# Squared-ReLU MLP of a hybrid decoder layer: up-projection by Strassen's scheme, in three passes over the tokens

## The chip, the cores and the metric

The kernel runs on one core of a Trainium2 chip. The metric is the device time of one execution in microseconds, smaller is better. Engines that matter here: PE (TensorE, matmuls; each has its own weight load, PEld), DVE (VectorE), ACT (ScalarE), POOL (GpSimd), and SP, whose queue issues nearly all DMA transfers. Each engine runs its own list of instructions in order, and semaphores tie the lists together.

## The reference, cut to what matters

2048 prompt tokens (with 16 meta tokens in front that are dropped from the output) and 8 sample tokens go through one layer of width D = 1024. The change touches the last two lines of the layer and the final norm:

```python
h = h + jnp.concatenate([y_hg, y_cv], axis=-1) @ w_out
hn2 = _rmsnorm(h, norm2_g)
h = h + jnp.square(jax.nn.relu(hn2 @ w_up)) @ w_down      # w_up 1024x4096, w_down 4096x1024
y = _rmsnorm(h, final_g)
```

All of it is fp32. The kernel keeps to that precision by splitting each operand into a high part that the matmul takes exactly (type fp32r) and the remainder, and by adding three products: high x high, high x low, low x high. So one fp32 block product of 128 x 128 weights costs three matmuls, each with its own weight load.

## The kernel before, in words

**Phase one** (to about 973 us of the span): input projection, gated recurrence, convolution and output projection, for four quarters of the tokens. Its last eight units are the output projection of quarter 3 (`plan_out(3)`, L746). Each unit's epilogue (`out_epilogue`, L1368) adds the residual to the sums in PSUM, and `out_store` (L1322) writes rows of h to DRAM (`hscr`), squares them on ACT and adds the squares on POOL; a few small matmuls then give the mean square of each token.

**Phase two, the MLP** (`plan_mlp`, L705) works on two halves of the tokens: 1032 columns (1024 and the 8 samples) in three blocks of 344, then 1024 in two of 512. Activations lie transposed, features on partitions and tokens along the free dimension. D_FF is cut in eight chunks of 512. A chunk has four up units (8 slices of the inner dimension x 3 products x blocks) and eight down units (4 x 3 x blocks). Where the last chunk of a half is reached, `LASTB` (L703) cuts its blocks anew so that the finish of the first columns starts early.

The norm's token factor is not applied to the operand: since relu squared is homogeneous, the kernel multiplies the residual by the mean square instead (`acc_init`, L1460: `acc` starts as h times `msb`), adds the down products to it, and corrects in the final norm (`finish`, L1472: transposes on PE, squares on ACT, an inverse square root by small one-column DVE operations, two multiplications by gains, a store; `finish_last`, L1501, does the last two tiles). `up_epilogue` (L1586) makes relu and square and both halves of `hid`; `down_epilogue` (L1600) adds a PSUM unit to `acc` on DVE.

`h_prep` (L769) loads a slice of h, multiplies by the gain, and splits it (ACT high, DVE low) into `hT`. For the first half it is added to the background at the start of quarter 2's out units (L1414), for the second half behind the last up unit of the first half (L1660), ahead of that half's last down units.

**Weights** come in pieces of 1 MB (`w_of`, three buffers `wsp0` to `wsp2`). In the first half each piece is loaded raw, split (ACT high, POOL low, `split_to`, L631) and stored to DRAM (`kw`); in the second half it is reloaded split.

**Order.** Units are issued in the order of `plan`. Between the slices of a unit a scheduler (`Background`, `bg.step`) issues background steps: each generator (`h_prep`, `finish`, `acc_init`, ...) yields the engine that it needs next, and the step is taken up when a planner's model of the engines' times says that it is due. The order on each engine is thus fixed when the program is built.

## Time and profile before

| | us |
|---|---|
| median of 3 runs (lowest, highest) | 2449.05 (2447.9, 2450.72) |
| profiled execution | 2447.64 |
| its span | 2445.7 |
| PE busy | 2352.7 (96%) |
| DVE busy | 1171.4 (48%) |
| ACT busy | 683.4 (28%) |
| POOL busy | 520.7 (21%) |

How to read it: every instruction is recorded by one helper (L146), so groups are told apart by tile names (`ps` is PSUM, `act` and later `op0`, `op1`, `extra` hold the operands of the up-projection, `acc` the sums, `wsp` weights, `stat` and `kept` the small columns of an inverse square root). "out<-in" names what is written and read. Matmuls overlap, so a mean of 320 ns is the time from start to end of one, not the distance between two.

### The profile page before, as it was taken

Reading aid. Unit: us, or ns where it says so; the run is one execution under the profiler, and the core shown is the slowest. Engines: PE = TensorE matmul, PEld = TensorE weight load, DVE = VectorE, ACT = ScalarE, POOL = GpSimd, SP = SyncE. Lnnn points to the kernel's source line nnn. Section 1 sums busy time; section 2 is a strip of 40 time slices with the busy share of each in tenths; the row PEclk is TensorE's granted clock in tenths of the full one; section 3 lists DMA queues with packets and bytes.
Section 4 is the critical chain, followed back from the end, with each engine's and each line's share of the span. In section 5 each row is a group of like instructions: output and inputs, shape, how many; then the busy total and the mean of one; then the engine's idle time right before and its main releaser. Section 6 shows DMA issues by size and latency. Waiting matters only on the chain.

```text
span 2445.7 us, 31621 instructions
## 1 busy us (share of the span) xinstructions
PE 2352.7 (96%) x13000; PEld 2100.7 (86%) x13000; DVE 1171.4 (48%) x2003; ACT 683.4 (28%) x1239; POOL 520.7 (21%) x326
## 2 busy tenths in 40 slices
PE   8887898989999999999999999999999999999998
PEld 8887777967887788999999999999888888888887
DVE  6798978587659653523323323326722212222225
ACT  6443644463345333212212211213301100100112
POOL 4562414442237112222212212211000000000000
PEclk9889999999999999999999999999999999999999
DMA  9665454944474468644444444448522222222222
GB/s 300 201 215 175 153 192 139 307 165 167 168 248 159 144 233 294 232 155 141 130 150 135 138 147 140 136 153 304 216 94 95 94 98 92 98 92 98 92 93 97
DMA packets 159221, 396.27 MB, mean 162 GB/s; under 512 B 8772, under 2 KB 107657, under 8 KB 125278
## 3 DMA queue, kind: packets, MB, share of 16 engines
q1 hardware_dynamic: 158934, 394.00, 47.5%
q8 instruction: 102, 1.67, 0.3%
q14 instruction: 41, 0.34, 0.0%
q10 hardware_dynamic: 144, 0.26, 0.0%
HBM read 265.91 MB, written 128.79 MB: 161 GB/s over the span
## 4 chain that ended last, share of the span: by engine, by line
PE 73%; DVE 6%; ACT 1%; DMA 1%; issue 0%; POOL 0%; SPq 0%; ACTq 0%; POOLq 0%; DVEq 0%
PE ps L146 73%; DVE ps L146 3%; DVE stat L146 1%; ACT scr L146 0%; DVE kept L146 0%; DMA scr<-xscr 0%; DVE I L146 0%; DMA wsp<-kw 0%; POOL scr L146 0%; DVE act L146 0%; DVE scr L146 0%; DVE glu L146 0%; DVE B L146 0%; DVE xn L146 0%; ACT act L146 0%
## 5 line engine op out<-in xcount | busy, mean ns | idle before, releaser
L146 PE MATMUL ps<-act,wsp 128*128 128x512 f32 (+5 forms) x7704 | 1504.6, 354 | 8.8 <-POOL wsp L146 4.3
L146 PEld LDWEIGHTS ps<-act,wsp 128*128 128x128 f32 x7704 | 1284.4, 191 | 171.2 <-POOL wsp L146 4.9
L146 PE MATMUL ps<-hid,wsp 128*128 128x344 f32 (+4 forms) x3864 | 713.0, 345 | 1.6 <-DMA wsp<-kw 1.6
L146 PEld LDWEIGHTS ps<-hid,wsp 128*128 128x128 f32 x3864 | 646.4, 188 | 64.0 <-issue 1.8
L146 DVE TENSOR_TENSOR acc<-ps,acc 128x1032 f32<-128x1032 f32 (+5 forms) x160 | 162.0, 1013 | 467.4 <-PE ps L146 467.3
L146 POOL TENSOR_TENSOR wsp<-raw,wsp 128x1024 fp32r<-128x1024 f32 (+1 forms) x98 | 235.6, 2404 | 611.4 <-ACT wsp L146 575.8
L146 DVE TENSOR_TENSOR xn<-xn 128x1032 f32<-128x1032 f32 (+3 forms) x68 | 80.3, 1180 | 509.3 <-ACT hid L146 509.3
L146 ACT ACTIVATE xn<-ps 128x1032 f32<-128x1032 f32 (+5 forms) x74 | 69.2, 935 | 835.1 <-PE ps L146 832.3
L146 POOL TENSOR_TENSOR scr<-scr 128x512 f32<-128x512 f32 x172 | 227.8, 1325 | 266.8 <-ACT scr L146 241.8
L146 DVE SCALAR_TENSOR_TENSOR ps<-glu,cw,ps 128x512 f32<-128x512 f32 x292 | 219.5, 752 | 5.8
L146 ACT ACTIVATE wsp<-raw 128x1024 fp32r<-128x1024 f32 (+1 forms) x98 | 101.6, 1037 | 299.8 <-PE ps L146 216.0
L146 DVE TENSOR_TENSOR hid<-xn,hid 128x1032 fp32r<-128x1032 f32 (+3 forms) x68 | 133.5, 1963 | 2.3
L146 ACT ACTIVATE scr<-glu,cw 128x512 f32<-128x512 f32 x188 | 125.7, 715 | 2.0 <-DVE glu L146 2.0
L146 DVE TENSOR_TENSOR scr<-ps,scr 128x512 f32<-128x512 f32 x48 | 32.8, 684 | 81.1 <-DMA scr<-xscr 55.8
L146 ACT ACTIVATE hid<-xn 128x1032 fp32r<-128x1032 f32 (+3 forms) x68 | 69.0, 1015 | 2.2
L146 ACT ACTIVATE junk<-ps 128x128 bf16<-128x128 f32 (+3 forms) x100 | 38.3, 383 | 108.4 <-PE ps L146 95.2
L146 POOL TENSOR_TENSOR fg<-fg 128x512 f32<-128x512 f32 x28 | 36.6, 1307 | 97.7 <-ACT fg L146 97.7
L146 DVE RECIPROCAL I<-B 128x512 f32<-128x512 f32 (+1 forms) x16 | 54.0, 3378 | 0.5
L146 DVE SCALAR_TENSOR_TENSOR stat<-stat,kept 128x4 f32<-128x4 f32 (+4 forms) x144 | 41.8, 291 | 3.3
L146 DVE TENSOR_TENSOR act<-scr,act 128x512 fp32r<-128x512 f32 (+1 forms) x30 | 23.7, 791 | 37.7 <-ACT act L146 37.6
L146 PE MATMUL ps<-ident,scr 128*128 128x128 f32 (+1 forms) x148 | 22.1, 282 | 17.8 <-ACT scr L146 17.8
L146 DVE TENSOR_TENSOR stat<-stat,kept 128x4 f32<-128x4 f32 (+4 forms) x144 | 37.6, 261 | 3.4
(189 smaller groups left out, 1192.1 us busy)
## 6 DMA issues: line engine op xcount, KB each, us to landing
wsp<-kw SPq DMA_DIRECT2D x167, 1024.0 KB, 4.8
kw<-wsp SPq DMA_DIRECT2D x96, 1024.0 KB, 5.6
raw<-in_w_up_dram SPq DMA_DIRECT2D x32, 512.0 KB, 6.5
raw<-in_w_down_dram SPq DMA_DIRECT2D x32, 512.0 KB, 6.0
raw<-in_w_in_dram SPq DMA_DIRECT2D x24, 512.0 KB, 7.9
out_dram<-xn SPq DMA_DIRECT2D x18, 512.0 KB, 4.4
scr<-xscr SPq DMA_DIRECT2D x32, 256.0 KB, 7.2
hscr<-scr SPq DMA_DIRECT2D x32, 256.0 KB, 7.1
```

The costliest lines, as they stand in the source:

```text
L146: return fn(*args, **kw)
```

## The change

**Three passes.** Tokens go in three passes of 688, 688 and 680 columns (`T0`, `PN`), each split in two halves of 344 or 340 columns. D_FF goes in 16 groups of 256.

**Seven products.** In a group, w_up is a 2 x 2 matrix of blocks (two halves of D, two halves of the group's 256 columns) and the tokens' operand another (two halves of D, two halves of the pass). Strassen's scheme (Winograd's form) replaces eight block products by seven, P1 to P7, each 4 slices x 3 matmuls. S1 to S4 are sums of blocks of w_up, T1 to T4 sums of blocks of h. `up_epilogue` puts the four output blocks together in `cst` by DVE additions (P5 is held in PSUM bank 1 until P7), then makes relu and square and `hid`.

**Weight sums every pass.** Per group `up_prep` loads four raw blocks, makes four sums, and splits seven blocks: seven high parts on ACT, five low parts on DVE, two on POOL, into a ring of nine slots. `up_first` does this for the first group during the out units of quarter 3; six of its steps come after the out-projection. Down weights are split in pass 0 (ACT, POOL), stored, and reloaded in passes 1 and 2.

**Token sums.** `h_prep(p, i)` (i = 0 to 3) loads slices i and i + 4 of the pass, makes the four sums and splits seven blocks into single buffers (`op0`, `op1`, `extra`), through two stages (`bst0`, `bst1`) that it shares with `up_prep`. For pass 0 it is added at the start of quarter 3's out units, i = 2 and 3 go through `acc`, and need the memory of phase one; for passes 1 and 2 it waits for the last product of the pass before.

**Order.** Middle groups alternate products and down units (U0 D0 U1 D1 ... U6 D6 D7, the D's of the group before). The first group of a pass has seven products in a row; the last one ends with 13 down units in a row.

**Residual and norm.** The first group's down units are copied to `acc` by ACT. The residual h times mean square is added in the background during the pass (`residual`: a load, a POOL multiplication, a DVE addition for each of eight slices). Mean squares go through DRAM (`mscr`), and the column for the final norm is gathered by 20 small transfers (`eps_cols`). All six finish tiles of a pass wait for the last down unit of the pass; in the last pass the last down units run in two sweeps of 424 and 256 columns, and `finish_last` does the last two tiles.

```diff
+    NPASS, NG = 3, DFF // 256
+    T0 = [0, 680, 1368]
+    PROMPT = [680, 688, 680]
+    PN = [688, 688, 680]
...
+    PRODUCTS = [("P1", "A11", 0, B11), ("P5", "S1", 1, T1), ("P6", "S2", 2, T2), ("P3", "S4", 0, B22),
+                ("P7", "S3", 2, T3), ("P2", "A12", 0, B21), ("P4", "A22", 2, T4)]
...
+                (4, 0, "dve", total("S3", "A11", "S1", ALU.subtract)), (4, 0, "dve", total("S1", "S1", "A22", ALU.add)),
+                (4, 0, "act", hi("A11")), (5, 0, "dve", total("S2", "S1", "A11", ALU.subtract)),
+                (5, 0, "dve", total("S4", "A12", "S2", ALU.subtract)), (5, 0, "act", hi("A22")),
+                (6, 0, "dve", lo("A11", V)), (6, 0, "act", hi("A12")), (7, 0, "pool", lo("A22", G)),
+                (7, 1, "act", hi("S4")), (8, 1, "dve", lo("S4", V)), (9, 2, "act", hi("S3")),
+                (9, 0, "pool", lo("A12", G)), (10, 2, "dve", lo("S3", V)), (11, 5, "act", hi("S1")),
+                (12, 5, "dve", lo("S1", V)), (13, 6, "act", hi("S2")), (13, 6, "dve", lo("S2", V))]
...
+    def up_first():
+        steps = up_prep(0)
+        late = (20, 21, 13, 14, 15, 17)
+        got = yield from take(bstage, 2)
+        for n_ in [n_ for n_ in range(len(steps)) if n_ not in late] + list(late):
+            if n_ == late[0]:
...
+                bstage.give(*got)
+                yield from until(("mix",))
...
+    def h_prep(p, i):
+
+        n = PN[p] // 2
+        yield from until(*[("h", q, d) for q in quarters(p) for d in (i, i + 4)])
+        if p == 0:
+            yield from region(i // 2, 4)
+        else:
+            yield from until(("up", p - 1))
+        if p == 0 and i < 2:
+            raws = yield from take(xns, 2)
...
+        st_ = yield from take1(bstage)
...
+        lo_scaled(B11, r[B11], g)
+        lo_(T1, s1)
+        lo_(T2, s2)
+        done.add(("bop", p, i, 0))
...
+                G.tensor_tensor(t[:, 0:n], t[:, 0:n], msb[:, 0:n], ALU.mult)
...
+                V.tensor_tensor(acc[:, k, 0:n], acc[:, k, 0:n], t[:, 0:n], ALU.add)
...
+            yield from until(("emm",), *[("res", p, k) for k in range(K8)])
...
+            r_ = yield from rsqrt(ss, 1, 1.0 / D, parts=n, eps=emm[:n, p, i:i + 1])
...
+            if name == "P1":
+                S.activation(c11, src, AF.Copy)
+            elif name == "P6":
+                V.tensor_tensor(c21, src, c11, ALU.add)
+                V.tensor_tensor(c12, held, c21, ALU.add)
+            elif name == "P3":
+                V.tensor_tensor(c12, src, c12, ALU.add)
+                ready(c12, a, 1)
+            elif name == "P7":
+                V.tensor_tensor(c21, src, c21, ALU.add)
+                V.tensor_tensor(c22, held, c21, ALU.add)
+                ready(c22, b, 1)
...
+                if g == 0:
+                    bg.wait(done, ("bop", p, i, idx // 3))
+                for wl, xl in ((0, 0), (0, 1), (1, 0)):
+                    mctx.t = 0.0
+                    T.matmul(ps[:, bank_, 0:n], lhsT=w[:, wl, i * P:(i + 1) * P], rhs=bop(i, xl, idx)[:, 0, 0:n],
+                             start=(i == 0 and wl == 0 and xl == 0), stop=(i == 3 and wl == 1))
...
+        def down(p, g, d, bl, outs, w):
+            m = len(outs)
+            n = (bl[1] - bl[0]) // m
+            mctx.e = "pe"
+            for k in range(2):
+                for wl, xl in ((0, 0), (0, 1), (1, 0)):
+                    lhs = w[:, wl, k * P:(k + 1) * P]
+                    for h in range(m):
+                        mctx.t = 0.0
+                        c0_ = bl[0] + h * n
+                        T.matmul(outs[h], lhsT=lhs, rhs=hid[g % 2][k][:, xl, c0_:c0_ + n],
+                                 start=(k == 0 and wl == 0 and xl == 0), stop=(k == 1 and wl == 1))
...
+                    bg.until(lambda: all(("fin", p - 1, i) in done for i in range(6)))
+                S.activation(a, view_, AF.Copy)
+                done.add(("acc", p, d))
+            else:
+                V.tensor_tensor(a, view_, a, ALU.add)
...
+            seq += U_(0, range(7))
+            for g in range(1, NG):
+                ds = [D_(g - 1, d) for d in range(K8)]
+                us = U_(g, range(7))
+                if g == 1:
+                    seq += us[0:3] + [x for i in range(4) for x in (ds[i], us[3 + i])] + ds[4:]
+                elif g == NG - 1:
+                    seq += [us[0], ds[0], us[1], us[2], ds[1], us[3], us[4], ds[2], us[5], us[6]] + ds[3:]
+                else:
+                    seq += [x for i in range(7) for x in (us[i], ds[i])] + ds[7:]
+            bls = [whole] if p < NPASS - 1 else [(0, 424), (424, 680)]
+            seq += [D_(NG - 1, d, bl) for bl in bls for d in range(K8)]
```

What the change does to the order, at three places. First DVE where the out-projection ends. `scr<-ps` is the eviction of an out unit; `act<-xn` before, and `op0<-xn` after, are low parts of the up operand; `bst` are stages, `ups` and `wsp` weights of the first group, `fg<-ps` the mean square of quarter 3. Before:

```order
L146 TENSOR_TENSOR scr_111<-ps_96,scr_111 128x512 [waits DMAHW0_49,PE_49]
L146 TENSOR_TENSOR scr_111<-ps_96,scr_111 128x512 [waits DMAHW3_49,PE_49]
L146 TENSOR_TENSOR scr_111<-ps_96,scr_111 128x512 [waits DMAHW6_49,PE_49]
L146 TENSOR_TENSOR scr_111<-ps_96,scr_111 128x512 [waits DMAHW1_49,PE_49,Pool_49]
L146 SCALAR_TENSOR_TENSOR act_83<-xn2_91,vec_70,act_83 128x1032 [waits Activation_49]
L146 SCALAR_TENSOR_TENSOR act_83<-xn0_89,vec_70,act_83 128x1032 [waits Activation_49]
L146 SCALAR_TENSOR_TENSOR act_83<-xn1_90,vec_70,act_83 128x1032 [waits DMAHW4_49,Activation_49]
L146 SCALAR_TENSOR_TENSOR act_83<-xn3_92,vec_70,act_83 128x1032 [waits DMAHW7_49,Activation_49]
```

After:

```order
L146 TENSOR_TENSOR scr_115<-ps_93,scr_115 128x512 [waits DMAHW3_49,PE_49]
L146 TENSOR_TENSOR ups3_7385<-raw0_84,ups3_7385 128x512 [waits Activation_49]
L146 TENSOR_TENSOR wsp1_87<-raw0_84,wsp1_87 128x512 [waits DMAHW5_49,Activation_49]
L146 SCALAR_TENSOR_TENSOR bst0_7386<-xn3_114,ng2_78,bst0_7386 128x344 [waits DVE_49,Activation_49,Pool_49]
L146 SCALAR_TENSOR_TENSOR bst0_7386<-xn1_90,vec_70,bst0_7386 128x336 [waits DMAHW2_49,DVE_49]
L146 TENSOR_TENSOR bst0_7386<-kept_76,bst0_7386 128x8 [waits Activation_49]
L146 TENSOR_SCALAR fg_91<-ps_93 1x512 [waits PE_49]
L146 TENSOR_TENSOR wsp1_87<-raw1_85,wsp1_87 128x512 [waits Activation_49]
L146 SCALAR_TENSOR_TENSOR bst1_7387<-xn0_89,ng2_78,bst1_7387 128x344 [waits Activation_49]
L146 SCALAR_TENSOR_TENSOR bst1_7387<-xn2_113,vec_70,bst1_7387 128x336 [waits DMAHW4_49,DVE_49]
L146 TENSOR_TENSOR bst1_7387<-kept_76,bst1_7387 128x8 [waits Activation_49]
L146 SCALAR_TENSOR_TENSOR op0_82<-xn3_114,vec_70,op0_82 128x344
```

The four preparations that stood in one piece behind the last eviction are replaced by a chain of sums and splits, of which the first low part of the first slice is the last row shown, and weight remainders stand among them.

Second, DVE at the end of the first half (before) and of pass 0 (after). `stat` and `kept` are the inverse square root of a finish tile, `xn<-ps` its multiplication by gains. Before:

```order
L146 SCALAR_TENSOR_TENSOR kept_76<-stat_75,kept_76 128x1 [waits DVE_49]
L146 SCALAR_TENSOR_TENSOR stat_75<-stat_75,kept_76 128x1 [waits DVE_49]
L146 TENSOR_TENSOR stat_75<-stat_75,kept_76 128x1 [waits DVE_49]
L146 SCALAR_TENSOR_TENSOR kept_76<-stat_75,kept_76 128x1 [waits DVE_49]
L146 SCALAR_TENSOR_TENSOR stat_75<-stat_75,kept_76 128x1 [waits DVE_49]
L146 TENSOR_TENSOR stat_75<-stat_75,kept_76 128x1 [waits DVE_49]
L146 TENSOR_TENSOR acc_7675<-ps_96,acc_7675 128x384 [waits PE_49]
L146 SCALAR_TENSOR_TENSOR kept_76<-stat_75,kept_76 128x1 [waits DVE_49]
L146 TENSOR_TENSOR kept_76<-kept_76,rs2_78 128x1 [waits DVE_49]
L146 SCALAR_TENSOR_TENSOR xn1_90<-ps_96,kept_76,fg_93 128x512 [waits DMAHW6_49,DVE_49,Pool_49]
L146 SCALAR_TENSOR_TENSOR xn1_90<-ps_96,kept_76,fg_93 128x512
```

After:

```order
L146 SCALAR_TENSOR_TENSOR kept_76<-stat_75,kept_76 128x1 [waits DVE_49]
L146 TENSOR_TENSOR stat_75<-stat_75,kept_76 128x1
L146 SCALAR_TENSOR_TENSOR bst1_7387<-raw0_84,ng2_78,bst1_7387 128x344 [waits DMAHW4_49,Activation_49]
L146 SCALAR_TENSOR_TENSOR bst1_7387<-raw1_85,vec_70,bst1_7387 128x344 [waits DMAHW5_49,DVE_49]
L146 SCALAR_TENSOR_TENSOR stat_75<-stat_75,kept_76 128x1
L146 SCALAR_TENSOR_TENSOR kept_76<-stat_75,kept_76 128x1
L146 TENSOR_TENSOR stat_75<-stat_75,kept_76 128x1 [waits DVE_49]
L146 SCALAR_TENSOR_TENSOR stat_75<-stat_75,kept_76 128x1 [waits DVE_49]
L146 SCALAR_TENSOR_TENSOR kept_76<-stat_75,kept_76 128x1 [waits DVE_49]
L146 SCALAR_TENSOR_TENSOR xn1_90<-ps_93,kept_76,fg_91 128x512 [waits DVE_49,PE_49]
L146 SCALAR_TENSOR_TENSOR xn1_90<-ps_93,kept_76,fg_91 128x512 [waits PE_49]
L146 SCALAR_TENSOR_TENSOR op1_83<-raw0_84,vec_70,op1_83 128x344 [waits Activation_49]
```

Before, adds of the last down units (`acc<-ps`) stand among the small operations; after, sums for the next pass's operand (`bst1<-raw`, `op1<-raw`) stand there, and all adds of the pass are ahead of them.

Third, PE at the end of the program. `ident,acc` are the transposes of finish tiles. Before:

```order
L146 MATMUL ps_96<-hid0_7669,act_83 128x256 [waits DVE_49]
L146 MATMUL ps_96<-hid0_7669,act_83 128x256 x2
L146 MATMUL ps_96<-hid1_7670,act_83 128x256 x3
L146 MATMUL ps_96<-hid2_7671,act_83 128x256 x3
L146 MATMUL ps_96<-hid3_7672,act_83 128x256 x3
L146 MATMUL ps_96<-ident_66,acc_7675 128x128
L146 MATMUL ps_96<-ident_66,acc_7675 128x128 [waits DVE_49]
L146 MATMUL ps_96<-ident_66,acc_7675 128x128 x7
L146 MATMUL ps_96<-ident_66,acc_7675 128x128 [waits DVE_49]
L146 MATMUL ps_96<-ident_66,acc_7675 128x128 x2
L146 MATMUL ps_96<-ident_66,acc_7675 128x128 [waits DVE_49]
L146 MATMUL ps_96<-ident_66,acc_7675 128x128
L146 MATMUL ps_96<-ident_66,acc_7675 128x128 [waits DVE_49] x2
```

After:

```order
L146 MATMUL ps_93<-ident_66,acc_7718 128x128 [waits DVE_49]
L146 MATMUL ps_93<-ident_66,acc_7718 128x128 x3
L146 MATMUL ps_93<-ident_66,acc_7718 128x128 [waits DVE_49]
L146 MATMUL ps_93<-ident_66,acc_7718 128x128 x3
L146 MATMUL ps_93<-ident_66,acc_7718 128x128 [waits DVE_49]
L146 MATMUL ps_93<-ident_66,acc_7718 128x128 x3
L146 MATMUL ps_93<-ident_66,acc_7718 40x128 [waits DVE_49]
L146 MATMUL ps_93<-ident_66,acc_7718 40x128 x3
L146 MATMUL ps_93<-ident_66,acc_7718 40x128 [waits DVE_49]
L146 MATMUL ps_93<-ident_66,acc_7718 40x128 x3
L1991 UNCONDITIONAL_BRANCH
```

Before, the last matmuls with `hid` are followed by 16 transposes, the rest of the last two tiles. After, no matmul with `hid` is near the end: the rows shown end with the eight transposes of a tile of 128 tokens and the eight of the tile of 40 tokens, half a tile at a time behind a wait for DVE.

## Rows read from the trace of the kernel before

**Rows 1.** The page: busy share of each engine; chain that ended last, by engine.
```profile
PE 2352.7 (96%) x13000; PEld 2100.7 (86%) x13000; DVE 1171.4 (48%) x2003; ACT 683.4 (28%) x1239; POOL 520.7 (21%) x326
...
PE 73%; DVE 6%; ACT 1%; DMA 1%; issue 0%; POOL 0%; SPq 0%; ACTq 0%; POOLq 0%; DVEq 0%
```

**Rows 2.** Windows: stretch, length, busy us (x instructions) of PE, PEld, DVE, ACT, POOL, granted clock, DMA.
```profile
970.00:2430.00 1460.00, 1457.94 (x7961) 1326.70 (x7960) 462.98 (x587) 236.94 (x290) 159.15 (x67) 1.00 0.40 135
1100.00:1300.00 200.00, 200.00 (x1269) 200.00 (x1268) 61.90 (x36) 39.00 (x38) 42.14 (x18) 1.00 0.45 139
1800.00:2000.00 200.00, 200.00 (x866) 162.13 (x865) 42.86 (x35) 16.69 (x16) 0.00 (x0) 1.00 0.27 95
```

**Rows 3.** Groups of PE by form: operands, shape xcount, busy us, mean ns, idle before.
```profile
L146 PE MATMUL ps<-act,wsp 128*128 128x344 f32 x2232 | 355.0, 320 | 0.0
L146 PE MATMUL ps<-hid,wsp 128*128 128x512 f32 x1416 | 329.4, 394 | 0.0
```

**Rows 4.** Timeline of ACT, first half: start us, length us; two up units in a row.
```profile
1205.48 1.03 ACT L146 ACTIVATE xn<-ps 128x1032 f32<-128x1032 f32 x1 [8.28 <-PE ps L146]
...
1216.84 1.03 ACT L146 ACTIVATE xn<-ps 128x1032 f32<-128x1032 f32 x1 [8.28 <-PE ps L146]
```

**Rows 5.** Timeline of ACT, second half: two up units in a row.
```profile
1925.77 1.02 ACT L146 ACTIVATE xn<-ps 128x1024 f32<-128x1024 f32 x1 [8.98 <-PE ps L146]
...
1936.86 1.02 ACT L146 ACTIVATE xn<-ps 128x1024 f32<-128x1024 f32 x1 [8.98 <-PE ps L146]
```

**Rows 6.** Groups of DVE by form, 970 us to the end.
```profile
L146 DVE TENSOR_TENSOR hid<-xn,hid 128x1032 fp32r<-128x1032 f32 x31 | 90.2, 2908 | 1.1
L146 DVE TENSOR_TENSOR acc<-ps,acc 128x1032 f32<-128x1032 f32 x56 | 68.9, 1231 | 213.1 <-PE ps L146 213.1
...
L146 DVE TENSOR_TENSOR hid<-xn,hid 128x1024 fp32r<-128x1024 f32 x31 | 38.0, 1225 | 1.1
...
L146 DVE SCALAR_TENSOR_TENSOR xn<-ps,kept,fg 128x512 f32<-128x512 f32 x28 | 19.7, 746 | 1.3 <-DVE kept L146 0.5
...
L146 DVE TENSOR_TENSOR acc<-ps,acc 128x384 f32<-128x384 f32 x16 | 8.8, 553 | 11.5 <-PE ps L146 11.5
...
L146 DVE SCALAR_TENSOR_TENSOR stat<-stat,kept 128x1 f32<-128x1 f32 x42 | 6.6, 157 | 1.0
```

**Rows 7.** Groups of POOL by form, whole span: weight splits of 512 columns.
```profile
L146 POOL TENSOR_TENSOR wsp<-raw,wsp 128x512 fp32r<-128x512 f32 x4 | 5.1, 1283 | 8.3 <-ACT wsp L146 8.2
```

**Rows 8.** DMA issues: count, KB each, us from issue to landing.
```profile
out_dram<-xn SPq DMA_DIRECT2D x18, 512.0 KB, 4.4
...
xn<-hscr SPq DMA_DIRECT2D x16, 512.0 KB, 8.1
```

**Rows 9.** Timeline of DVE where phase one ends and the MLP begins.
```profile
973.39 0.69 DVE L146 TENSOR_TENSOR scr<-ps,scr 128x512 f32<-128x512 f32 x1 [4.92 <-PE ps L146]
974.00 5.94 DVE L146 SCALAR_TENSOR_TENSOR act<-xn,vec,act 128x1032 fp32r<-128x1032 f32 x4
```

**Rows 10.** Timeline of PE where the first half of the tokens ends.
```profile
1705.93 0.85 PE L146 MATMUL ps<-hid,wsp 128*128 128x264 f32 x5 [1.59 <-DMA wsp<-kw]
```

**Rows 11.** Timeline of DVE there: two finish tiles in a row.
```profile
1715.23 0.15 DVE L146 TENSOR_TENSOR stat<-stat 128x1 f32<-128x1 f32 x1
...
1719.53 0.15 DVE L146 TENSOR_TENSOR stat<-stat 128x1 f32<-128x1 f32 x1
```

**Rows 12.** Timeline of PE around a gap in phase one.
```profile
805.55 0.66 PE L146 MATMUL ps<-ident,I 128*128 128x128 f32 x4 [4.50 <-DVE I L146]
```

**Rows 13.** Windows of that gap and of the 4 us behind it.
```profile
800.00:806.00 6.00, 1.50 (x10) 0.98 (x8) 5.82 (x12) 0.20 (x1) 2.63 (x3) 1.00 0.44 172
806.00:810.00 4.00, 4.00 (x17) 3.44 (x16) 3.78 (x7) 0.80 (x2) 0.00 (x0) 0.57 0.00 0
```

**Rows 14.** Timeline of PE at the end.
```profile
2429.17 2.98 PE L146 MATMUL ps<-hid,act 128*128 128x256 f32 x24
2431.99 1.69 PE L146 MATMUL ps<-ident,acc 128*128 128x128 f32 x14
```

More of the change, by code (lines that the diff above doesn't have):

```diff
@@ L1337, in out_store @@
                 if d == K8 - 1:
-                    half, i0 = q // 2, 4 * (q % 2)
                     if q == 0:
@@ new lines, in eps_cols @@
+        def eps_cols():
+            yield "pool"
+            G.memset(emm, 1.0)
+            yield from until(*[("st", q) for q in range(NQ)])
+            yield "sp"
+            for p in range(NPASS):
+                for i, c0_, n in tiles_of(p):
+                    m = min(n, PROMPT[p] - c0_)
+                    a = T0[p] + c0_
+                    SP.dma_start(emm[0:m, p, i:i + 1], mscr[:, a:a + m].rearrange("o p -> p o"))
+                    if m < n:
+                        SP.dma_start(emm[m:n, p, i:i + 1], mscr[:, SEQ:SEQ + NS].rearrange("o p -> p o"))
+            yield "dve"
+            V.scalar_tensor_tensor(out=emm, in0=emm, scalar=EPS, in1=emm, op0=ALU.mult, op1=ALU.mult)
+            done.add(("emm",))
```

639 lines of the change are left out of this document (396 added, 243 removed).

## The prediction

> **What bounds the kernel now.** The page comes first [rows 1]: PE is busy 96% of the span, DVE 48%, and the chain that ended last is 73% PE. Then the windows [rows 2]: from 970 to 2430 us PE is busy 1457.9 of 1460 us at granted clock 1.00 (2.4 GHz), while DVE has 463 us. The MLP is one unbroken stream of matmuls, and only its length counts; DVE and ACT have slack on average. The groups by form [rows 3] show no idle time before these matmuls, so I read their price from the cadence, not from their 320 ns of latency. An up unit of 72 matmuls of 344 columns comes every 1216.84 − 1205.48 = 11.36 us, which is 157.8 ns each [rows 4]; one of 48 of 512 columns every 11.09 us, 231.0 ns each [rows 5]. Both are 0.45 to 0.46 ns per column: columns are paid, not instructions.
>
> The stream runs from the eviction of the last out-projection unit at 973.4 [rows 9] to 2429.17 + 2.98 = 2432.15 [rows 14]: 1458.8 us. The profiled execution took 2447.64 us, 1.4 below the median; its span is 2445.7, so 1.9 lie around it.
>
> **Part by part: the stream.** Before: 4248 matmuls of 344 (670.3 us), 2952 of 512 (681.9), and 600 narrower ones of the last units, 185,280 columns at 0.459 ns (85.0): 1437.2. The other 21.6 of the 1458.8 are 1.6 of waiting for a weight piece [rows 10] and mostly transposes, some 0.12 each [rows 14]. After: 3 passes x 16 groups x (7 products x 12 + 8 down units x 12) = 8640 matmuls: 5760 of 344 (908.9), 2784 of 340 at 156.0 (434.2), and 48 each of 424 and 256 (15.0): 1358.1. **−79.1 us**, an eighth of the up columns.
>
> A rule speaks against this. The Trainium skill, "TensorE: Matmul & The Clock Gate", section "Back-to-back issue gap", gives about 81 ns for sustained 128-column pairs of weight load and matmul, and 131 ns for 512. By it (109 ns at 344, an estimate on a straight line between these) the stream would go from about 910 to 942 us, +32 for −79. The trace disagrees with 157.8 and 231.0.
>
> **The start of the MLP.** Before, the operands of the first up unit are ready when the out-projection ends: DVE's last four preparations take 5.94 us in one piece at 974.0 [rows 9], and PE goes on. After, h_prep cannot take its stages until up_first gives them back, and DVE comes to it only behind the last evictions. From there to the operand that the last quarter of P1 needs, DVE has 24 scalar_tensor_tensors of 336 or 344 columns, 11 tensor_tensors of 344, 5 operations of 512 columns and 10 of 8 columns. By [rows 6] 344 columns cost about 0.515 (384 cost 0.553, 1032 cost 1.231), a scalar_tensor_tensor of 344 about 0.57 (0.746 at 512), 512 columns 0.69, a small one 0.16: 13.7 + 5.7 + 3.5 + 1.6 = 24.5 us against 1.9 us of PE for P1. Moreover the four loads for i = 2, 3 stand on SP behind two stores of down weights, and these wait for POOL's split behind ACT's first preparations, at about 18; a load lands some 8 us later [rows 8] and leaves about 8 us of DVE. That makes some 33, less 1.9, and a little for the second group's sums, which wait for a stage: **+32** (24 by DVE alone, 40 if a second load queues).
>
> **The two pass boundaries.** Before, the second half's operands lie ready and finish tiles spread among adds; the whole boundary cost 1.6 us [rows 10]. After, the next pass may overwrite its operands only once U6 of group 15 is done, and D0 needs a bank pair that the last finish tile gives back. Between the last add of a pass and that tile's gains DVE has, in its order, 16 scalar_tensor_tensors and 21 tensor_tensors of 344, 9 of 512, 12 gains and 78 one-column operations: 9.1 + 10.8 + 6.2 + 9.0 + 12.2 = 47.3 us [rows 6]. These are dependent chains: a tile alone took 4.3 us before [rows 11], so some 3 more. PE has 10 products (18.9) and 48 transposes (5.8) to run meanwhile: 24.7. The first pass also splits down weights on POOL, where a 1032-column subtraction on DVE took 2.91 for 1.23 [rows 6]; that puts DVE late before it begins. **+28** (20 to 36) and **+26** (18 to 34), each with 5.8 of transposes besides.
>
> **Inside the groups.** A group is 7 x 1.89 + 8 x 1.89 = 28.4 us of PE. DVE has 9 sums and remainders of 512 (6.2), 7 adds of products (3.6), 4 remainders of hid (2.1) and 8 adds of 688 columns at 0.875 (7.0): 18.9. POOL's splits in the first pass are at most 7.8, half of 1.28 for 256 columns [rows 7]; even if DVE stood still for all of them, 26.7 fits in 28.4. The residual adds 8 POOL products (1.7 each, by the same row) and 8 DVE adds per pass; they are hidden unless DVE is already late. **+3** (0 to 12) for products that come out of step.
>
> **Clock.** In phase one a gap of 4.5 us [rows 12] was followed by a stretch at granted clock 0.57 [rows 13], mostly at the 1.2 GHz level: 0.43 of 4 us, 1.7 us, are lost. From 970 to 2430 there is none [rows 2]. The new stalls hold gaps of that size at three places, more than one at each: **+6** (0 to 12).
>
> **Tail.** From the last hid matmul to the end of the span it is now 13.5 us. After, the last sweep has 48 matmuls of 256 columns (5.6 us), and DVE four finish tiles (15), eight adds (3.4) and the last two tiles (6.5): 25 us. The last store lands 4.4 later [rows 8]: 25 − 5.6 + 4.4 = **24** (18.5 to 26.5).
>
> **Sum.** 973.4 + 1358.1 + 32 + (28 + 5.8) + (26 + 5.8) + 2.9 (transposes in the last sweep) + 3 + 6 = 2441.0 for the last matmul; + 24 + 1.9 = **2467**, +19 on 2447.6. The saving is real and is more than spent where DVE prepares operands that PE needs at once.
>
> **Rivals.**
> *The boundaries hide more.* If every low end holds (24, 20, 18, no low clock, no wait in groups, tail 18.5), the time is 2467 − 38 = 2429, faster. For it: DVE is only 48% busy, independent operations overlap a little, and before, finish tiles cost PE nothing. Against it: the order on DVE is fixed and its 47 us are counted. It decides for faster once the three stalls together are below some 62 us instead of 86.
> *Waits in the steady state.* If each group's adds come 1 us late, 48 groups give +48 less the 3 counted: 2512. For it: held bank 1 ties two products to one add, and POOL beside DVE is dear [rows 6]. Against it: 18.9 of 28.4. It decides if DVE with POOL's share passes 28.4.
> *Price by instruction.* If a matmul's price were one of instructions, 840 more at 157.8 would be +133 instead of −79: 2679. The 512-column cadence [rows 5] excludes nearly all of it: the slope between [rows 4] and [rows 5] leaves 8 ns per instruction. The rule of the Trainium skill above points this way.
> *The stream alone.* If preparation is covered entirely, 2447.6 − 79 = 2369: the change would do all that its count promises. Against it: h_prep cannot begin before the last product by its own condition.
>
> **How the numbers follow.** Forecast case (2443 to 2500) 0.66, hidden boundaries 0.17, waits 0.13, the stream alone 0.03, price by instruction 0.01. The range leaves out the two last, half of the waits and some of the hidden case: 2430 to 2505. About 0.2% (5 us) is what a measurement can tell: faster 0.18 (below 2442.7), same 0.12, slower 0.70.
>
> **What would show it.** In the changed profile: 157 to 158 ns per matmul in mid-pass; PE idle of some 30 us behind the out-projection with DVE as releaser; two stretches of some 25 us at pass starts where DVE is full and PE is not; low clock there; mid-pass PE at 100%. I am wrong if those stretches are short, if mid-pass PE is below 97%, or if the last matmul ends far from 2441.

## The result, and the profile after

The changed kernel takes 2520.27 us (median of 4 runs, 2515.5 to 2524.6) against 2449.89: a ratio of 1.029 [1.026, 1.031], slower by 70 us. The forecast was slower by 19, with 2505 as its upper end; the direction was right and the size was not. The profiled execution took 2517.8 us, its span is 2516.1.

The page after, against [rows 1]: busy share of each engine, PE and its granted clock in 40 slices, the chain that ended last.

```profile
PE 2317.9 (92%) x13790; PEld 2166.6 (86%) x13790; DVE 1704.1 (68%) x3129; ACT 1056.1 (42%) x2230; POOL 655.1 (26%) x511
...
PE   9887889989999996899999977999999889999996
...
PEclk9898999999999998899999997999999989999998
...
PE 52%; DVE 12%; issue 6%; DMA 4%; ACT 3%; POOL 3%; SPq 1%; DVEq 0%; POOLq 0%; ACTq 0%
```

PE's share of the chain falls from 73% to 52%. Each slice is 63 us long. Behind the first 15, PE's slices dip at three places, the starts of the three passes, and at the end. Windows after, against [rows 2]: group 0 of pass one (passes count from one here, groups from 0 to 15); its groups 5 to 8; start of pass two; its groups 5 to 14; start of pass three.

```profile
985.00:1035.00 50.00, 22.43 (x85) 18.95 (x84) 34.53 (x74) 22.62 (x56) 5.09 (x5) 0.61 0.31 88
1155.00:1270.00 115.00, 112.18 (x706) 111.17 (x707) 77.95 (x114) 50.58 (x112) 40.91 (x40) 1.00 0.49 152
1494.00:1579.00 85.00, 56.78 (x312) 52.89 (x311) 57.91 (x161) 41.50 (x90) 8.11 (x5) 0.80 0.34 113
...
1670.00:1950.00 280.00, 280.00 (x1781) 280.00 (x1780) 175.32 (x278) 100.31 (x196) 25.45 (x20) 1.00 0.38 113
1998.00:2075.00 77.00, 55.59 (x314) 52.64 (x313) 55.12 (x158) 39.05 (x86) 8.13 (x5) 0.80 0.36 109
```

In the middle of pass two PE is as full as before. Its timeline there, units of 12 matmuls (start, length), as [rows 4] was read:

```profile
1755.20 2.06 PE L146 MATMUL ps<-op,wsp 128*128 128x344 f32 x12
...
1770.31 1.89 PE L146 MATMUL ps<-op,ups 128*128 128x344 f32 x11
```

Eight units, 96 matmuls, start in 15.11 us: 157.4 ns per matmul of 344 columns, against 157.8 in [rows 4]. A group of the third pass repeats every 28.0 us, 155.6 ns per matmul of 340. The stream is 5760 x 157.4 + 2784 x 155.6 ns and 15 us for the wide and narrow ones of the last group: 1354.8 us. **The saving on PE is there in full.** What is left of a stretch when its matmuls are taken off at this cadence I call lost; transposes, and the useless matmuls of e11 and e12, count as lost too. A stretch runs from the first matmul of an up unit to that of another; the starts of passes two and three are their first two groups, with 48 transposes (e1 and e3 have none there). "First group" is group 0 of pass one. All in us, each from one profiled execution:

| kernel | first matmul | lost: first group | rest of pass 1 | start of pass 2 | rest of 2 | start of pass 3 | rest of 3 | last group | last matmul |
|---|---|---|---|---|---|---|---|---|---|
| after | 985.5 | 36.4 | 18.8 | 43.8 | 6.7 | 36.0 | 6.2 | 2.7 | 2490.9 |
| e1 no finish | 986.1 | 35.8 | 19.0 | 18.8 | 6.2 | 17.2 | 3.8 | 2.7 | 2444.5 |
| e2 no preparation | 985.0 | 35.5 | 15.9 | 31.7 | 7.2 | 27.6 | 6.1 | 2.6 | 2466.3 |
| e3 neither | 987.6 | 36.4 | 18.2 | 13.2 | 4.4 | 8.1 | 6.0 | 2.7 | 2431.4 |
| e4 eight products | 983.9 | 18.8 | 4.1 | 20.3 | 1.2 | 15.5 | −0.5 | 2.7 | 2491.2 |
| e5 ng2 moved | 982.0 | 37.1 | 18.3 | 42.5 | 8.4 | 36.4 | 6.2 | 2.6 | 2488.4 |
| e6 low part on ACT | 983.3 | 37.5 | 34.6 | 41.8 | 6.6 | 37.4 | 6.1 | 2.6 | 2504.7 |
| e7 loads at the start | 985.4 | 26.0 | 28.9 | 43.5 | 7.6 | 37.2 | 6.0 | 2.6 | 2492.0 |
| e8 sums later | 987.8 | 35.5 | 18.5 | 40.7 | 6.4 | 37.8 | 5.8 | 2.6 | 2489.9 |
| e9 rounding on POOL | 988.0 | 35.0 | 15.5 | 43.5 | 6.6 | 35.8 | 5.8 | 2.7 | 2487.6 |
| e10 no residual | 989.5 | 34.9 | 15.7 | 40.1 | 0.9 | 37.0 | 0.0 | 2.6 | 2475.5 |
| e11 filled gaps | 986.6 | 35.4 | 18.9 | 38.3 | 4.9 | 34.6 | 3.4 | 2.6 | 2479.4 |
| e12 all moves | 982.0 | 24.9 | 20.0 | 35.9 | 5.9 | 35.6 | 2.5 | 2.6 | 2464.2 |
| e13 down weights ready | 987.6 | 30.4 | 2.1 | 37.3 | 8.8 | 36.7 | 4.7 | 2.6 | 2464.8 |

The first column scatters: in the kernels that keep phase one as the change has it, the first matmul comes between 983.3 and 989.5 us.

Rows that show the waits. DVE at the end of phase one, against 973.39 in [rows 9]:

```profile
980.90 0.69 DVE L146 TENSOR_TENSOR scr<-ps,scr 128x512 f32<-128x512 f32 x1 [1.89 <-PE ps L146]
```

PE at the start of the MLP (idle before and who ended it), then at the start of pass two:

```profile
1004.01 0.65 PE L146 MATMUL ps<-op,ups 128*128 128x344 f32 x1 [11.49 <-ACT op L146]
...
1026.44 3.81 PE L146 MATMUL ps<-op,wsp 128*128 128x344 f32 x12 [6.52 <-DVE cst L146]
...
1527.73 3.81 PE L146 MATMUL ps<-op,ups 128*128 128x344 f32 x12 [6.36 <-DVE cst L146]
...
1554.04 3.81 PE L146 MATMUL ps<-hid,wsp 128*128 128x344 f32 x12 [6.79 <-DVE xn L146]
```

The last line is D0 of pass two; its releaser, on DVE, is the gain of the last finish tile:

```profile
1552.59 1.40 DVE L146 SCALAR_TENSOR_TENSOR xn<-ps,kept,fg 48x512 f32<-48x512 f32 x2
```

### The profile page after: what moved, and what is told of

Same layout as the page of the kernel before. It is cut to its first block, busy times and chain, and to the rows that moved or that the text cites. A ratio compares the mean times of both kernels' runs of the same rounds, so it can differ in the third digit from the quotient of the medians.

```text
span 2516.1 us, 37234 instructions
## 1 busy us (share of the span) xinstructions
PE 2317.9 (92%) x13790; PEld 2166.6 (86%) x13790; DVE 1704.1 (68%) x3129; ACT 1056.1 (42%) x2230; POOL 655.1 (26%) x511
## 4 chain that ended last, share of the span: by engine, by line
PE 52%; DVE 12%; issue 6%; DMA 4%; ACT 3%; POOL 3%; SPq 1%; DVEq 0%; POOLq 0%; ACTq 0%
PE ps L146 52%; DVE ps L146 2%; DMA junk<-in_w_down_dram 2%; DVE stat L146 2%; POOL wsp L146 1%; ACT cst L146 1%; SPq L146 1%; DVE op L146 1%; DMA bst<-in_w_up_dram 1%; DVE raw L146 1%; DVE acc L146 1%; DVE xn L146 1%; DVE cst L146 1%; POOL ups L146 1%; ACT wsp L146 1%
## 5 line engine op out<-in xcount | busy, mean ns | idle before, releaser
L146 PE MATMUL ps<-op,wsp 128*128 128x512 f32 (+6 forms) x5427 | 1068.9, 352 | 33.9 <-DVE cst L146 11.4
L146 PEld LDWEIGHTS ps<-op,wsp 128*128 128x128 f32 x5427 | 897.4, 195 | 137.7 <-DVE cst L146 11.1
L146 PE MATMUL ps<-hid,wsp 128*128 128x344 f32 (+1 forms) x4536 | 769.5, 321 | 34.1 <-DVE xn L146 13.8
L146 DVE TENSOR_TENSOR acc<-ps,acc 128x688 f32<-128x688 f32 (+3 forms) x368 | 313.2, 851 | 278.1 <-PE ps L146 277.5
L146 ACT ACTIVATE cst<-cst 128x344 f32<-128x344 f32 (+1 forms) x384 | 188.3, 490 | 507.3 <-DVE cst L146 501.2
L146 PE MATMUL ps<-op,ups 128*128 128x344 f32 (+1 forms) x2013 | 358.3, 326 | 34.0 <-ACT op L146 15.2
L146 PEld LDWEIGHTS ps<-op,ups 128*128 128x128 f32 x2013 | 330.9, 193 | 39.5 <-ACT op L146 16.4
L146 DVE TENSOR_TENSOR cst<-ps,cst 128x344 f32<-128x344 f32 (+1 forms) x336 | 171.1, 509 | 30.6 <-PE ps L146 27.1
L146 DVE TENSOR_TENSOR hid<-cst,hid 128x344 fp32r<-128x344 f32 (+1 forms) x192 | 104.6, 545 | 52.6 <-ACT hid L146 51.6
L146 POOL TENSOR_TENSOR wsp<-raw,wsp 128x1024 fp32r<-128x1024 f32 (+1 forms) x34 | 78.7, 2314 | 79.6 <-ACT wsp L146 68.1
```

The lines of the kernel that those rows point to most:

```text
L146: return fn(*args, **kw)
```

## The experiments

The kernel before was run on the same chip each time: 2451 to 2453 us, 1 to 3 above the 2449.89 of the result. The changed kernel was not run again beside the experiments, so a difference of 3 us or less from its 2520.27 says little.

**e1, e2, e3: what the pass starts are made of.** e1 leaves out the finish tiles of passes one and two:

```diff
-                    bg.until(lambda: all(("fin", p - 1, i) in done for i in range(6)))
...
-            elif g == NG - 1 and d == K8 - 1:
+            elif p == NPASS - 1 and g == NG - 1 and d == K8 - 1:
```

e2 leaves out the operands of passes two and three (those of pass one are used again); e3 does both:

```diff
-                if p < NPASS - 1:
-                    for i in range(4):
-                        bg.add(h_prep(p + 1, i), 1)
+                for i in range(4):
+                    for a_ in range(3):
+                        done.add(("bop", p + 1, i, a_))
```

> The changed kernel without the finish tiles of passes 0 and 1 (their rows of y are not written; the wait of the next pass's first down unit on them goes with them). Theory (DVE's list of operations between the passes sets the boundaries, which cost 49.6 and 42.3 us): 21 to 24 us of DVE and 5.3 of transposes leave each boundary, so each falls by 15 to 22 and the time by 30 to 44, to 2476-2490. Rival (only the preparation of operands counts, finish tiles lie beside it): under 10 us less in all, 2508 or more.

> The changed kernel with the operands of pass 0 used in passes 1 and 2 too (no preparation for these passes; their products are of the wrong tokens). Theory (DVE's list): 24 us of DVE leave each boundary and its first product waits for nothing; what is left is the finish tiles' chain against 10 products, some 8 to 15 us a boundary: 65 to 80 less, 2438-2455. Rival (the wait of the first down unit on the last finish tile decides alone): the boundaries fall by 10 each, about 2500.

> Both left out: no finish tiles in passes 0 and 1 and no operands for passes 1 and 2. Theory: only the wait behind the second group's weight sums is left, some 6 us a boundary: 80 less, about 2440. If the two parts add up, e3's gain is the sum of e1's and e2's; if they stand in one queue where either fills it, e3's gain is less than the sum. Rival (boundaries cost by the low clock or by transfers): over 2470.

Measured: 2473.1, 2495.6 and 2455.1 us. By the table the finish tiles are worth 25.0 and 18.8 us at the two starts, the operands 12.1 and 8.4, both together 30.6 and 27.9. So the work of DVE there is the cause of most of it. Of what the tiles are worth, 5.8 us are their 48 transposes on PE, by the prediction's price; the rest, 19.2 and 13.0, is about one and a half times the operands' share, as the work is: between the last add and the last gain, the tiles take 21.2 us of DVE by the prediction's terms (9.0 + 12.2), and the operands 16 scalar_tensor_tensors and 10 tensor_tensors, 14.3 us. (The prediction has 21 tensor_tensors there; of the 22 in the trace, 12 are adds of products and remainders of `hid`. Its 9 operations of 512 columns are weight sums and low parts of the second group.) e2 was a miss: 25 us less where 65 to 80 were expected, near its rival, since D0 waits for the last tile with or without the operands before it. PE in e2:

```profile
1537.65 3.81 PE L146 MATMUL ps<-hid,wsp 128*128 128x344 f32 x12 [6.86 <-DVE xn L146]
```

e3 came 15 us above its forecast. One long wait stays at each of its starts, 9.33 us in pass two and 4.1 in pass three. PE, then DVE, in pass two:

```profile
1512.64 3.81 PE L146 MATMUL ps<-op,ups 128*128 128x344 f32 x12 [9.33 <-DVE cst L146]
```

```profile
1504.78 0.69 DVE L146 TENSOR_TENSOR raw<-bst,raw 128x512 f32<-128x512 f32 x1 [8.13 <-DMA bst<-in_w_up_dram]
```

DVE is free, but its weight sums for the second group stand in its order ahead of the add that PE waits for, and they wait for loads. Behind the first limit lay a second.

**e4: eight products in the new frame.** The three passes, their operands, finish tiles and residual stay; C11 = A11 B11 + A12 B21 and so on takes the place of Strassen's sums and adds.

```diff
-    UP = ["A11", "A12", "A22", "S1", "S2", "S4", "S3"]
-    PRODUCTS = [("P1", "A11", 0, B11), ("P5", "S1", 1, T1), ("P6", "S2", 2, T2), ("P3", "S4", 0, B22),
-                ("P7", "S3", 2, T3), ("P2", "A12", 0, B21), ("P4", "A22", 2, T4)]
+    UP = ["A11", "A12", "A22", "S1"]
+    PRODUCTS = [("c11a", "A11", 0, B11), ("c11b", "A12", 0, B21), ("c12a", "A11", 1, B12), ("c12b", "A12", 1, B22),
+                ("c21a", "S1", 2, B11), ("c21b", "A22", 2, B21), ("c22a", "S1", 0, B12), ("c22b", "A22", 0, B22)]
```

(S1 holds A21 there.)

> Three passes, 16 groups and the background residual kept, but eight block products a group instead of seven: no sums of weights or tokens, four blocks split instead of seven on either side, products accumulated in PSUM, no additions of products on DVE. PE gets 48 more products (+90.6 us by the measured 157.4 ns). Theory (Strassen's extra work on DVE and ACT is what the boundaries, the start and pass 0 cost): the start falls from 41 to about 18, the boundaries from 50 and 42 to about 25 each, pass 0's waits from 18 to 5: 75 less, so 2510-2550 in all. Rival (three passes cost it, whatever the products): the losses stay and the time is 2590-2615.

Measured: 2519.55 us, 1.028 [1.027, 1.030], the time of the changed kernel. Windows of e4: group 0, groups 2 to 14 of pass one, start of pass two.

```profile
984.00:1018.00 34.00, 20.72 (x100) 18.40 (x99) 8.75 (x18) 10.81 (x25) 4.02 (x5) 0.75 0.49 137
1048.00:1442.00 394.00, 394.00 (x2500) 394.00 (x2500) 170.04 (x189) 137.87 (x323) 131.45 (x139) 1.00 0.47 146
1490.00:1556.00 66.00, 54.47 (x341) 53.55 (x339) 33.25 (x113) 30.62 (x68) 8.88 (x6) 0.92 0.44 143
```

576 matmuls more are 90.3 us of stream (384 x 157.4 + 192 x 155.6 ns); the losses of its line in the table sum to 62.1 for 150.6, 88.5 less. So its theory held, and this is the sum of the whole case: **in this frame the product saved costs as much in waits as it gives on PE, and the 70 us are the price of the frame** (three passes with their operands, finish tiles, residual and 16 groups), which e4 pays too. Against the kernel before, in the terms of the prediction, the span of e4 (2516.3 us) is 70.6 us longer: 40.5 in waits and transposes (62.1 for 21.6), 11.7 behind the last matmul with `hid`, 10.5 ahead of the first one of the MLP, 7.9 in the stream itself. What seven products would do in the frame of the kernel before was not tried.

**e5: phase one.** The change has one small operation there, ng2 = −g2 on 128x8; e5 moves it behind phase one.

```diff
-                V.tensor_scalar(ng2, g2, -1.0, None, ALU.mult)
...
         steps = up_prep(0)
+        yield "dve"
+        V.tensor_scalar(ng2, g2, -1.0, None, ALU.mult)
```

> The one small operation of the change that stands in phase one (ng2 = -g2, a 128x8 multiplication on DVE) is moved behind phase one, to the start of the weight preparation; nothing else changes, and the planner then gives phase one its old order. Theory: this operation alone made phase one 7.5 us longer by another order of the work; the last eviction of the out-projection returns from 980.9 to 973 to 975 us and the time falls to 2513 (2510 to 2516). Rival: phase one is longer because of the DMA traffic or the buffers of the change; then the eviction stays at 980 to 982 and the time at 2518 to 2523.

Measured: 2518.3 us; the last eviction falls at 977.37 (980.90 above). At 454 us PE stands 6.1 us behind the kernel before in the changed kernel and 0.1 in e5, so the operation did change the order of that part. e12, which moves it too, stands 0.1 behind there and ends at 977.39; the kernels that keep it stand 3.1 to 7.7 behind and end between 978.7 and 984.9. But e5 gets behind again from 500 us on and ends 4.0 late. Half of the theory held. The rest, in the part where the preparation of the first up weights runs beside phase one, was not tried.

**e6, e9, e13: why pass one loses 1 us per group.** DVE in a group of pass one, then PE:

```profile
1153.60 0.81 DVE L146 TENSOR_TENSOR ups<-raw,ups 128x512 fp32r<-128x512 f32 x1 [2.44 <-ACT ups L146]
1154.33 0.86 DVE L146 TENSOR_TENSOR acc<-ps,acc 128x688 f32<-128x688 f32 x1
```

```profile
1155.34 2.13 PE L146 MATMUL ps<-hid,wsp 128*128 128x344 f32 x12 [1.67 <-DVE acc L146]
```

The down unit waits for the add that frees its banks; that add stands on DVE behind the low part of an up weight, and this idles 2.44 us for ACT's rounding. Only pass one splits down weights, on ACT and POOL. e6 lets ACT write a copy in place of the low part; e9 rounds on POOL; e13 reads all down weights ready-made from memory (wrong ones in the right shape), which leaves out the split and with it the raw loads and the stores.

```diff
 e6
-                    G.tensor_tensor(w[:, 1], r, w[:, 0].bitcast(F32), ALU.subtract)
+                    S.activation(w[:, 1], r, AF.Copy)
 e9
-                    S.activation(w[:, 0], r, AF.Copy)
+                    G.tensor_copy(w[:, 0], r)
 e13
-                    SP.dma_start(flat32(dslots[j % 4]), down_w[8 * g + d])
...
+                SP.dma_start(flat32(dslots[j % 4]),
+                             list(kept_w.values())[at // 4][:, 512 * (at % 4):512 * (at % 4) + 512])
...
-                if p == 0:
+                if False:
```

> In the first pass the low part of each down weight piece is written by ACT (a copy, 0.4 us) and not by POOL's subtraction; the low part's value is thus left out (it holds the rounded value of the whole instead). Theory: POOL's subtractions stretch DVE's operations beside them, and this makes the first pass lose about 1 us per group at D0 (20 us in all, 18 of it over the other passes' mid groups); the mid groups of the first pass then take 28.3 to 28.5 us as in passes two and three, and the time falls to 2504 (2500 to 2509). Rival: the first pass waits for the down weights themselves, which arrive from memory in another form and need two more steps; then its groups still take 29 to 30 us and the time stays at 2516 to 2522.

> In the first pass the high part of each down weight piece is rounded by POOL and not by ACT; all else stays. Theory, formed after the experiment with POOL's splits: in the first pass ACT's copies of the down weights stand in front of its copy of the next up weight's high part; DVE's low part of that weight waits for it, and behind it, in DVE's fixed order, the add that frees the banks for the next down unit. With the copies gone from ACT the groups 3 to 14 of the first pass take 28.3 to 28.7 us for 28.5 to 30.3, and the time falls by 8 to 13 us to 2509 (2505 to 2513). Rival: the weights simply arrive too late in the first pass, or POOL beside DVE is the price after all; then the groups take 29 us or more and the time is 2517 to 2535.

> The down weights of all passes are read from a buffer of weights that phase one has left in memory in the split form (the wrong weights, in the right shape), so that the first pass makes no split on ACT and POOL and no store: this leaves the splitting of the down weights out. Theory: the splitting as a whole, ACT's rounding and POOL's subtraction together, is what the first pass loses; groups 7 to 14 of the first pass then take 28.3 to 28.6 us, group 15 loses under 2 us, the start loses some 8 us less since no store stands in front of the rows' loads, and the time is 2499 (2493 to 2505). Rival: the first pass loses something else (the up weights' sums, loads beside the stream); then its groups still take 28.8 us or more, and the time is 2507 or more.

Measured: 2532.9, 2515.1 and 2490.9 us. Windows of groups of pass one in e6, e9 and e13 (after: 112.18 of 115 on PE):

```profile
1155.00:1270.00 115.00, 109.46 (x682) 108.43 (x681) 74.69 (x108) 56.60 (x136) 16.84 (x10) 0.99 0.46 143
```

```profile
1155.00:1270.00 115.00, 111.74 (x707) 111.01 (x706) 81.26 (x113) 40.02 (x80) 59.55 (x77) 1.00 0.49 156
```

```profile
1146.00:1260.00 114.00, 114.00 (x726) 114.00 (x725) 77.84 (x113) 41.25 (x81) 11.97 (x8) 1.00 0.42 112
```

e6 refutes POOL as the only cause: with its subtractions gone and ACT busier, 16 us more are lost. e9 was a miss: it gains 3.3 us in the rest of the pass, and the time falls by 5; POOL is busy 59.55 us then, and DVE beside it takes 81.26 for 77.95. e13 gained more than its forecast of 2499: the rest of the pass loses 2.1 us for 18.8, the first group 6.0 less, and the start of pass two 6.5 less. **The splitting of the down weights, the same amount as in the kernel before, is what pass one pays**, on ACT and POOL together; how much on each, and how much by the loads and stores that go with it, stays open. The Trainium skill, "Perfetto Trace Analysis", section "Optimizing Scalar/DVE Operations", warns that POOL and DVE share a read port, so that moving work between them "might not help". No run here moves work between these two; in e9 POOL takes work over from ACT, and the 3.3 us that DVE then takes longer point the same way.

**e7: the start.** The first down weights' load and split come ahead of the fourth product (the code counts from 0) and not of the first; the small column loads for the last norm, 19 of them, come in group 2.

```diff
-        bg.add(eps_cols(), 4)
...
-                    d_load(1)
-                    d_split(1)
-                    d_load(3)
...
+            if kind == "U" and p == 0 and g == 0 and d == 3:
+                d_load(1)
+                d_split(1)
+                d_load(3)
+            if kind == "U" and p == 0 and g == 2 and d == 0:
+                bg.add(eps_cols(), 4)
```

> Two moves at the start of the MLP: the load and split of the first down weight pieces is issued after the fourth product of the first group, so that the loads of the rows for the operands no longer stand behind their stores on SP; and the small column loads for the last norm are issued in group 2, not in front of the second group's up weights. Theory: the queue on SP holds the start (waits of 11.5 us for the last quarter's operands and of 6.5 us for the weight sums behind them); the first group then takes 38 to 43 us for 49.6, and the time falls to 2511 (2507 to 2514). Rival: DVE's own chain of operand preparation holds the start whatever is loaded when; then the first group still takes 47 us or more and the time is 2518 to 2523.

Measured: 2521.2 us, no gain. The first group does lose 10.4 less: in the changed kernel the loads of the rows for the last operands stand on SP behind two stores of down weights, and in e7 they go out 11.4 us earlier. But the column loads carried their price along: pass one loses 10.1 us more behind the first group, 7.5 of them in group 2. SP's queue after:

```profile
995.50 1.28 SPq L146 DMA_DIRECT2D down_w<-wsp  x2
...
997.87 1.88 SPq L146 DMA_DIRECT2D acc<-hscr  x4
...
1002.23 12.06 SPq L146 DMA_DIRECT2D emm<-mscr  x19
```

SP's queue in e7, and PE in its group 2:

```profile
986.47 1.75 SPq L146 DMA_DIRECT2D acc<-hscr  x4
...
1056.65 9.47 SPq L146 DMA_DIRECT2D emm<-mscr  x19
```

```profile
1073.17 3.81 PE L146 MATMUL ps<-op,ups 128*128 128x344 f32 x12 [4.38 <-DVE cst L146]
```

The 19 loads keep SP for 12.06 and 9.47 us, and the weight loads stand behind them, at either place.

**e8: order or amount at the pass starts.** The weight sums of the second group come behind the third product's add.

```diff
+                             ([a + 3] if G_ % NG == 0 and e != "sp" else []))
```

> In the first group of each pass, DVE's weight sums for the second group are issued behind the add of the third product, not in front of it (order of DVE alone; the amount of work is the same). Theory A, the order on DVE: the third product's add then no longer waits for weight loads, the waits of about 6.4 us on PE in the three first groups go, a part comes back at the start of the second group, and the time falls to 2510 (2505 to 2514). Theory B, the amount: at a pass start DVE has some 47 us of work for 25 of PE, so the end of the work is the same in any order; the waits move by one unit or two and the time stays at 2517 to 2523.

Measured: 2519.8 us: theory B. The wait of 6.36 us becomes one of 5.94 at the unit behind it, and the losses at the starts are 40.7 and 37.8. While DVE has all its work to do, the order is worth next to nothing; whether it would count with that work gone, as in e3, was not tried.

**e10: the residual.**

```diff
-                bg.add(residual(p), 6)
...
-            yield from until(("emm",), *[("res", p, k) for k in range(K8)])
+            yield from until(("emm",))
```

> The residual rows are left out (their loads, POOL's 24 products and DVE's 24 adds of 688 columns). Theory: they come when DVE has just caught up, and put it late at the third groups of passes two and three (5 us each) and at groups 4 to 6 of the first (about 1 us each); these losses go and the time is 2508 (2504 to 2512). Rival: the background adds are covered, and those groups are late from the pass start, for weight pieces; then the third groups still lose 4 to 5 us and the time is 2516 to 2522.

Measured: 2500.3 us, 20 less (16 in the profiled execution), more than the theory's 12. PE in group 3 of pass two, after, a wait for which the profile names no releaser; DVE there; then the window of groups 2 to 4 in e10:

```profile
1613.00 2.64 PE L146 MATMUL ps<-hid,wsp 128*128 128x344 f32 x12 [2.95 <-issue]
```

```profile
1609.23 0.86 DVE L146 TENSOR_TENSOR acc<-acc,xn 128x688 f32<-128x688 f32 x1
1611.43 0.69 DVE L146 TENSOR_TENSOR ups<-raw,ups 128x512 fp32r<-128x512 f32 x1 [1.34 <-ACT ups L146]
1612.04 0.87 DVE L146 TENSOR_TENSOR acc<-ps,acc 128x688 f32<-128x688 f32 x1
```

```profile
1575.00:1660.00 85.00, 85.00 (x542) 85.00 (x541) 50.64 (x82) 31.43 (x61) 7.62 (x6) 1.00 0.38 112
```

PE starts as the add of 1612.04 ends; ahead of it stand a low part that waits for ACT and, before that, an add of the residual (`acc<-acc`). Without the residual the rest of passes two and three loses 0.9 and 0.0 us for 6.7 and 6.2. So it is not background work: it falls on the groups behind a pass start, in which DVE is still late.

**e11: the clock.** 240 matmuls that nobody reads fill gaps of PE; `warm(p, m)` issues m of them.

```diff
+                if g == 0 and name == "P1" and i in (1, 2):
+                    warm(p, (8 if i == 1 else 48 if p == 0 else 24))
+                if g == 0 and name == "P7" and i == 0:
+                    warm(p, 24)
...
+                if p and g == 0 and d == 0:
+                    mctx.e = "pe"
+                    warm(p, 24)
```

> Matmuls whose result nobody reads are put into PE's gaps at the start of the MLP and at the two pass starts (8 to 48 at a place), into a bank that is free there; all else stays. Theory: the low clock behind the gaps costs some 14 us more than forecast; with the gaps filled the stretches at granted clock 0.5 go, and the time falls by 8 to 14 us to 2509 (2504 to 2513). Rival: PE at half clock only spends time for which DVE's work at the pass start would have kept it waiting; the clock stays high, but the waits grow by as much and the time is 2516 to 2523.

Measured: 2509.5 us, 10.8 less. A window behind the waits for finish tiles after, then the two pass starts of e11 (0.80 and 0.80 after):

```profile
1546.00:1560.00 14.00, 7.00 (x25) 6.44 (x26) 9.24 (x36) 1.95 (x4) 0.00 (x0) 0.51 0.27 102
```

```profile
1494.00:1574.00 80.00, 65.92 (x395) 62.51 (x394) 60.07 (x162) 41.38 (x90) 11.10 (x7) 0.91 0.39 130
1991.00:2066.00 75.00, 62.27 (x389) 59.14 (x389) 60.94 (x160) 38.61 (x85) 12.60 (x7) 0.95 0.39 120
```

After, PE ran at 1.2 GHz around its waits (granted clock 0.51), and the units behind the waits shown above take 3.81 us, where one in mid-pass takes 2.06. Filled, the granted clock rises to 0.91 and 0.95; the starts lose 6.9 us less, though the filling counts as lost, and the groups behind them 4.6. The filling also moves some transposes to an earlier group, so that not all of it is the clock's. The Trainium skill, "TensorE: Matmul & The Clock Gate", section "HAM oscillation — how this bites in real kernels", tells of the same: an engine that waits between short bursts starts each of them slow.

**e12: all moves together** (e5, e7 with the column loads spread one by one, e8, e9, e11).

> All moves that leave the work as it is, together: ng2 behind phase one, the rows' loads ahead of the first down weights, the small column loads spread over the groups from the sixth on, the weight sums later, the rounding on POOL, and the gaps filled. By the sum of the single experiments (3 + 10 + 10 + 2 and some of the clock's 10) the time is 2492 (2484 to 2500). Rival: at the pass starts DVE's amount of work decides and the single gains there are the same microseconds; then 2500 to 2512. By neither it comes below the kernel before, since the two pass starts keep some 60 of their 70 us.

Measured: 2491.8 us, 1.016 [1.014, 1.018]: the sum came out, though not by its terms. The start gave its 11.5 us and phase one 3.5; the rest of pass one gave nothing (20.0 for 18.8), while the start of pass two gave 7.9. It stays 39 us above the kernel before, with 71.5 us still lost at the two pass starts. Not tried was to spread the finish tiles among the last adds of a pass, as the kernel before has them.

## Why the prediction failed in size

The last matmul was forecast at 2441.0 and came at 2490.9. By the steps of the sum:

| step | forecast | measured | difference |
|---|---|---|---|
| end of phase one | 973.4 | 980.9 | +7.5 |
| stream | 1358.1 | 1354.8 | −3.3 |
| start of the MLP | 32 | 4.6 + 36.4 = 41.0 | +9.0 |
| start of pass two, with transposes | 33.8 | 43.8 | +10.0 |
| start of pass three, with transposes | 31.8 | 36.0 | +4.2 |
| inside the groups | 3 | 18.8 + 6.7 + 6.2 = 31.7 | +28.7 |
| last sweep's transposes | 2.9 | 2.7 | −0.2 |
| clock | 6 | lies in the stretches above | −6.0 |

The sum is +49.9. The end behind it was forecast with 24 + 1.9 and measured with 25.2 + 1.7.

- **The stream held**: −82 us by columns, no price by instruction.
- **Inside the groups was the step that failed.** The working added up DVE's operations (18.9 of 28.4 us), set POOL's beside them, and called them hidden. In groups 5 to 8 of pass one DVE is busy only 77.95 of 115 us, and PE still waits. What decides is the order: an add that frees banks stands behind an operation that waits for another engine. ACT's share, its rounding of the down weights among the rest, stood in no term. e13 shows 16.7 of the 18.8 us to be the split of the down weights with its loads and stores, work that cost nothing in the kernel before (200.00 of 200.00 us of PE in [rows 2]); e10 shows 12.0 of the other 12.9 to be the residual, which it called hidden "unless DVE is already late". It was late, behind each pass start. The prediction's own sign, mid-pass PE below 97%, was too coarse for this: 112.18 of 115 us are 97.5%, and so little adds up over a pass.
- **The pass starts had the right mechanism**: e1 to e3 and the wait of D0 for the last tile are as forecast. The size was short by 14 us, or 8 with the forecast's clock. From the last add to the last gain it took 58.5 us, and DVE was busy for 44.2 of them, where 47.3 had been counted; the other 14.3 it waited, 8.9 of them ahead of the second group's weight sums and low parts, for loads and for ACT. These waits, and that the sums stand ahead of an add, had not been counted. DVE's window there:

```profile
1495.50:1554.00 58.50, 30.32 (x159) 26.45 (x157) 44.18 (x139) 26.78 (x64) 2.93 (x2) 0.76 0.35 116
```

- **The start of the MLP** was named with its queue on SP, but costed at one load behind two stores. The 19 column loads behind them (the change's description says 20) were not counted, though SP issues them in one piece.
- **Phase one was taken as unchanged** and is 7.5 us longer, a move that the prediction did not cost at all. By e5 a part is the order that one small operation sets; the rest stays open.
- **The clock** was the right mechanism: 6 forecast; filling the gaps gave 10.8, not all of it the clock's.
- **The rivals.** The time fell near "waits in the steady state" (2512), and that is partly luck: 1 us in each of 48 groups was its price, and late adds did cost about 1 us a group, but in pass one alone; from group 5 on passes two and three lose nothing up to their last group. The hidden boundaries are refuted by the 43.8 and 36.0 us of the pass starts, the price by instruction by the cadence.

## What to carry to other kernels

Before a saving on the bounding engine is booked, follow one group instruction by instruction on every engine whose queue is in order, and ask at each wait what stands behind it; a busy share of 68%, as DVE's was in pass one, hides nothing by itself. Ask too which unchanged work lived under the time that is to be saved. And build the middle variant, with the new frame and the old count: e4 told in one run that seven products gain nothing on eight in this frame, and that the frame itself costs the 70 us.
